# Partial Strassen products in the gate and feed-forward projections of a two-layer encoder trunk

## The chip, the cores and the metric

The kernel runs on one core of one Trainium2 chip. The metric is device time in microseconds. Engines are named as the profile does: PE is TensorE, PEld its weight loads, DVE VectorE, ACT ScalarE, POOL GpSimd, SP SyncE, whose queue issues most DMAs.

## The reference

Two layers (`DEPTH = 2`) work on a sequence of 256 rows of width 2048, all in float32. In each layer one input projection feeds three attention branches, the branches are merged by gates that are computed from the layer's input, and a feed-forward part follows:

```python
h = x @ w_in[l]                                   # 2048 -> 4608, split into the heads of A, B, C
ya, yb, yc = ...                                  # three attentions
ga, gb, gc = jnp.split(jax.nn.sigmoid(x @ w_gate[l] + b_gate[l]), 3, axis=-1)     # 2048 -> 6144
mix = ga * (ya @ w_br_a[l]) + gb * (yb @ w_br_b[l]) + gc * (yc @ w_br_c[l])
x = layer_norm(DEEPNORM_ALPHA * x + mix @ w_out[l], ln1_g[l], ln1_b[l])
f_gate, f_up = jnp.split(x @ w_ffn_in[l], 2, axis=-1)                             # 2048 -> 2 x 5632
x = layer_norm(DEEPNORM_ALPHA * x + (jax.nn.silu(f_gate) * f_up) @ w_ffn_out[l], ln2_g[l], ln2_b[l])
```

## The kernel before

The 256 rows are two row tiles of 128. Each matrix product is cut into blocks of 512 output columns (`CW`) and k-tiles of 128; two k-tiles by 512 columns of a weight are one *unit* (`UK = 2`), a DMA of 512 KB into one of five `raw` buffers. `split_unit` cuts a unit into a rounded part and a rest, both of the type that TensorE takes at its full rate: ScalarE casts `raw` to `wh`, VectorE subtracts to get `wl`, with six buffers each. The activations are split the same way (`xh`, `xl`; `rh`, `rl`). A product of a row tile, a k-tile and a block is then three matmuls of 128x128 by 128x512: high by high, high by low, low by high. `gemm` does that for 16 k-tiles and two row tiles, 96 matmuls, into two PSUM banks `acc`, of which there are four; four more banks (`aux`) take transposes and small products.

The program is written with tiles, and a planner orders the instructions of each engine when the program is built: from the order in the text, the dependencies and durations that it estimates. An engine then works through its own list in that order. The attention work is written as generators in the list `side`; `pump` runs one step of the first of them after each unit of a `gemm`, and `drain` runs all that are left.

In the feed-forward part the first hidden block uses two plain `gemm` calls; the other ten blocks use `pair_gemm`, which makes the two column blocks (gate and up) together. Seen as two rows of tiles times two columns of blocks, k-tiles are taken four at a time as a 2x2 by 2x2 product, which Strassen's scheme does in seven products in place of eight. Before the change the first four k-tiles are one such *seven* with two k-tiles to a quarter, k-tiles 4 and 5 are a *seven* with one k-tile to a quarter, and the other ten are plain, `four`. The sums of x that the scheme needs are made once for a layer by `x_sums`; the sums of weights are made for each pair by VectorE:

```python
hub = act.tile([P, UK, CW], F32, tag=("rh3", "rl3")[turn[0]], name="hub")
nc.sync.dma_start(hub, block(src, k1, n2))
...
nc.vector.tensor_add(u, hub, w22)
nc.vector.tensor_add(hub, hub, w11)
nc.vector.tensor_add(u, u, w11)
nc.vector.tensor_add(u, u, w21)
```

A pair has seven banks, four of `acc` (`p3`, `p7`, `q5`, `q4`) and three of `aux` (`p1`, `p6`, `p2`); `todo` counts the products of each, 3 for `p1`, `p6`, `p7` and 13 for the others. At its end VectorE combines the banks to the four results (lines 660 to 667), ScalarE and VectorE make silu and the product, and TensorE transposes the hidden block (`hidTp`, line 136) for the product with `w_ffn_out`, which follows after each group of two or three blocks.

The gates are plain: for each of three branches and four blocks a `gemm` with `w_gate`, bias and sigmoid, and a `gemm` with the branch's weight (8, 4 and 4 k-tiles). In the last branch the mixed block is transposed (`mixTp`) right behind it. At the very start x comes in four chunks of 512 columns; each is loaded, transposed, cast by ScalarE and subtracted by VectorE when the first `gemm` comes to it, so the first product meets all four chunks in turn.

Of the kernel before, what the change touches and what calls it, by code (L numbers as in the profile page):

```python
# [33 lines left out]
def trunk_kernel(ctx: ExitStack, tc: tile.TileContext, x, w_in, sinks, lq1, lk1, lq2, lk2, diff_g,  # L34
# [16 lines left out]
    def split(h, l, src, scale=None):  # L51

        if scale is None:
            nc.scalar.copy(h, src)  # L54
            nc.vector.tensor_sub(l, src, h.bitcast(F32))  # L55
# [12 lines left out]

    def split_unit(raw):
# [3 lines left out]
        nc.scalar.copy(h[:, 0:n], raw)  # L73
        nc.vector.tensor_sub(l[:, 0:n], raw, h[:, 0:n].bitcast(F32))  # L74
        return h, l
# [17 lines left out]

    def gemm(src, kw0, nk, c0, lhs, tail=0):
# [24 lines left out]

    def tmp(name):  # L120
# [4 lines left out]

    def bcast(vec, c0, name):
        t = scr.tile([P, CW], F32, tag="bc", name=name, bufs=4)
        nc.gpsimd.dma_start(t, vec[c0:c0 + CW].partition_broadcast(P))
        return t
# [16 lines left out]
    def set_x(c, t, src):  # L146
# [3 lines left out]
        split(xh[c][t], xl[c][t], pv)  # L150

    def x_lhs(kt, t):
        c = kt // 4
        if xh[c][t] is None:
            x0 = [tmp("x0") for _ in range(NT)]
            for u in range(NT):
                nc.sync.dma_start(x0[u], x[0, u * P:(u + 1) * P, c * CW:(c + 1) * CW])
            for u in range(NT):
                set_x(c, u, x0[u])
# [15 lines left out]
    for layer in range(DEPTH):  # L175
# [48 lines left out]
        def v_heads(acc, col0, slots):  # L224
            for i, s in enumerate(slots):
                for t in range(NT):
                    nc.scalar.copy(s[:, t * P:(t + 1) * P], acc[t][:, col0 + i * P:col0 + (i + 1) * P])

# [111 lines left out]
        acc = gemm(wi, 0, 16, 1024, x_lhs)  # L340
# [10 lines left out]
        sink = const.tile([P, AQ], F32, tag="sink", name="sink")  # L351
        nc.sync.dma_start(sink, sinks[layer].partition_broadcast(P))
        nsink = const.tile([P, AQ], F32, tag="nsink", name="nsink")
        nc.vector.tensor_scalar_mul(nsink, sink, -1.0)

        lv = const.tile([P, 4, 64], F32, tag="lv", name="lv")
        for i, v in enumerate((lq1, lk1, lq2, lk2)):
            nc.sync.dma_start(lv[:, i, :], v[layer].partition_broadcast(P))
        lp = const.tile([P, 2, 64], F32, tag="lp", name="lp")
        nc.vector.tensor_mul(lp, lv[:, 0::2, :], lv[:, 1::2, :])  # L360
        ls = const.tile([P, 2], F32, tag="ls", name="ls")
        nc.vector.tensor_reduce(ls, lp, AX.X, ALU.add)
        le = const.tile([P, 2], F32, tag="le", name="le")
        nc.scalar.activation(le, ls, AF.Exp)
        lam = const.tile([P, 1], F32, tag="lam", name="lam")
        nc.vector.tensor_sub(lam, le[:, 0:1], le[:, 1:2])
        nc.vector.tensor_scalar_add(lam, lam, lam_init)

        gcol = const.tile([P, 1], F32, tag="gcol", name="gcol")
        nc.sync.dma_start(gcol, diff_g[layer].rearrange("(p o) -> p o", o=1))  # L370
        nc.vector.tensor_scalar_mul(gcol, gcol, 1.0 - lam_init)
# [3 lines left out]
        relb = const.tile([P, NHC, 3 * P], F32, tag="relb", name="relb")  # L375
        for h in range(NHC):
            raw = tmp("hank")[:, :SEQ]
            row = rel_bias[layer, h]
            nc.sync.dma_start(raw, bass.AP(row.tensor, row.offset + 129, [[1, P], [1, SEQ]]))
            nc.vector.tensor_add(relb[:, h, 0:P], raw[:, 0:P][:, ::-1], mask_b[:, 0:P])  # L380
            nc.vector.tensor_add(relb[:, h, P:3 * P], raw[:, ::-1], mask_b[:, P:3 * P])
# [3 lines left out]
        acc = gemm(wi, 0, 16, 0, x_lhs)  # L385
# [31 lines left out]

        mix = [[None] * NT for _ in range(NCH)]
        mixT = [None] * NCH
        for b, (wbr, nk, y0i) in enumerate(((w_br_a, 8, 0), (w_br_b, 4, 2), (w_br_c, 4, 3))):  # L420
# [4 lines left out]
            for c in range(NCH):  # L425
                bg = bcast(b_gate[layer], b * D + c * CW, "bg")
                acc = gemm(w_gate[layer], 0, 16, b * D + c * CW, x_lhs)
                gs = []
                for t in range(NT):
                    g = tmp("gate")  # L430
                    nc.vector.tensor_add(g, acc[t], bg)
                    nc.scalar.activation(g, g, AF.Sigmoid)
                    gs.append(g)
                if b == 0 and c == 0:
                    drain()
                acc = gemm(wbr[layer], 0, nk, c * CW, y_lhs)
                for t in range(NT):
                    if b == 0:
                        mix[c][t] = act.tile([P, CW], F32, tag=f"fb{c * NT + t}", name=f"mix{c}{t}")
                        nc.vector.tensor_mul(mix[c][t], gs[t], acc[t])  # L440
                    else:
                        nc.vector.tensor_mul(gs[t], gs[t], acc[t])
                        nc.vector.tensor_add(mix[c][t], mix[c][t], gs[t])
                if b == 2:
                    mixT[c] = ychunk(c)
                    for t in range(NT):
                        pv = transpose4(mix[c][t], "mixTp")
                        s = slice(t * P, (t + 1) * P)
                        split(mixT[c][0][:, :, s], mixT[c][1][:, :, s], pv)
# [66 lines left out]


        sums = {}
        turn = [0]

        def sum_tiles():
            pair = const.tile([P, 2, 4, P], F32R, tag="relb", name="sums")
            for i in range(6):
                yield act.tile([P, 4, P], F32R, tag=f"fa{i}", name="sums")
            for i in range(2):
                yield pair[:, i]
            while True:
                yield scr.tile([P, 4, P], F32R, tag="bc", name="sums", bufs=4)

        def x_sums(delay):  # L530


            yield from wait(delay)
            tiles = sum_tiles()
            for c in range(NCH):
                z = []
                for t in range(NT):
                    v = tmp("z").rearrange("p (k q) -> p k q", k=4)
                    nc.vector.tensor_add(v, xh[c][t].bitcast(F32), xl[c][t].bitcast(F32))
                    z.append(v)  # L540
                yield
                n = (2, 1, 0, 0)[c]
                if n:
                    a11, a12, a21, a22 = (v[:, j:j + n, :] for v in z for j in (0, n))
                    p = tmp("zs").rearrange("p (k q) -> p k q", k=4)
                    q = tmp("zs").rearrange("p (k q) -> p k q", k=4) if n == 2 else p[:, 2:4]
                    s1, s2, s3, s4 = p[:, 0:n], p[:, n:2 * n], q[:, 0:n], q[:, n:2 * n]
                    nc.vector.tensor_sub(s1, a21, a22)
                    nc.vector.tensor_sub(s3, a11, a21)
                    nc.vector.tensor_sub(s2, a11, s1)  # L550
                    yield
                    nc.vector.tensor_sub(s4, a12, s2)
                    parts = [p, q] if n == 2 else [p]
                else:
                    nc.vector.tensor_sub(z[0], z[0], z[1])
                    parts = [z[0]]
                got = []
                for v in parts:
                    h, l = next(tiles), next(tiles)
                    split(h, l, v)  # L560
                    got.append((h, l))
                    yield
                if n == 1:
                    nc.vector.tensor_sub(z[0][:, 2:4], z[0][:, 2:4], z[1][:, 2:4])
                    hl = next(tiles)
                    split(hl[:, 0:2], hl[:, 2:4], z[0][:, 2:4])
                    got.append((hl[:, 0:2], hl[:, 2:4]))
                    yield
                sums[c] = got

        def pair_gemm(src, n1, n2):

            bank = {}  # L580
            for k in ("p3", "p7", "q5", "q4"):
# [172 lines left out]
```

## Time and profile before

| | |
|---|---|
| time before, median of 3 runs | 2830.11 us (2830.01 to 2830.28) |
| the profiled execution: its own time | 2827.89 us |
| its span, first to last instruction | 2826.0 us |
| PE busy | 2791.0 us, 99%, 12660 matmuls and transposes |
| PEld busy | 2296.8 us, 81% |
| DVE busy | 1966.3 us, 70%, 2282 instructions |
| ACT busy | 1349.6 us, 48% |
| POOL busy | 60.7 us, 2% |
| DMA | 549.20 MB, 194 GB/s on average |

Busy time is the time in which at least one instruction of the engine runs; matmuls overlap, so a busy PE may still be waiting in part, and the distance between the starts of two matmuls says more. The profiled execution is one of its own and has its own time; the median is of other executions.

### The profile page before, as it was taken

To read this page: it belongs to the slowest core of one execution; us is meant where nothing else is said; L and a number is where in the kernel's file an instruction comes from. 1 tells how busy PE (TensorE), PEld (TensorE's weight loads), DVE (VectorE), ACT (ScalarE), POOL (GpSimd) and SP (SyncE) were. 2 spreads that over 40 slices of the span, in tenths; PEclk is the share of its full clock that TensorE was granted. 3 is DMA by queue.
4 is the path that set the end of the run, shared out by engine and by line. 5 is a ranking of instruction groups with operands and counts; after the bars stand their busy time and mean duration, and the time that the engine had idled before them with its cause. 6 is when DMAs were issued, how large, how long until landed. Compare 5 with 4: busy or idle time off the path is not lost. (4 is left out here: it accounts for less than half of the span.)

```text
span 2826.0 us, 33866 instructions
## 1 busy us (share of the span) xinstructions
PE 2791.0 (99%) x12660; PEld 2296.8 (81%) x12660; DVE 1966.3 (70%) x2282; ACT 1349.6 (48%) x1722; POOL 60.7 (2%) x110
## 2 busy tenths in 40 slices
PE   8999999999999999999999999999999999999998
PEld 6887888887888888888878888888878888888886
DVE  5656555566986877868776565555579779688686
ACT  4455444443554544545445454444435545455452
POOL 0000000000000000000000000000000000000000
PEclk9999999999999999999999999999999999999999
DMA  7555666665665666665764556666656656656564
GB/s 255 171 164 175 202 200 205 203 209 177 198 204 190 194 202 193 194 201 177 229 216 153 179 177 202 201 204 202 209 162 214 200 190 196 203 186 208 186 198 141
DMA packets 282660, 549.20 MB, mean 194 GB/s; under 512 B 19840, under 2 KB 21376, under 8 KB 282496
## 3 DMA queue, kind: packets, MB, share of 16 engines
q1 hardware_dynamic: 276096, 526.07, 58.1%
q0 software_dynamic: 6400, 20.98, 2.6%
q8 instruction: 99, 1.62, 0.2%
q14 instruction: 65, 0.53, 0.1%
HBM read 542.78 MB, written 4.19 MB: 194 GB/s over the span
## 5 line engine op out<-in xcount | busy, mean ns | idle before, releaser
L74 DVE TENSOR_TENSOR wl<-raw,wh 128x1024 fp32r<-128x1024 f32 x972 | 1182.6, 1223 | 718.0 <-ACT wh L73 713.6
L73 ACT CAST wh<-raw 128x1024 fp32r<-128x1024 f32 x972 | 1019.2, 1054 | 1239.1 <-PE acc L104 809.4
L102 PE MATMUL acc<-wh,xh 128*128 128x512 f32 x1472 | 582.2, 396 | 6.9 <-ACT xh L54 6.9
L103 PE MATMUL acc<-wl,xh 128*128 128x512 f32 x1472 | 575.8, 391 | 3.6 <-DVE wl L74 2.0
L104 PE MATMUL acc<-wh,xl 128*128 128x512 f32 x1472 | 576.2, 392 | 0.2 <-DVE xl L55 0.2
L103 PE MATMUL acc<-wl,rh 128*128 128x512 f32 x1216 | 474.3, 390 | 0.0
L102 PE MATMUL acc<-wh,rh 128*128 128x512 f32 x1216 | 473.8, 390 | 0.0
L104 PE MATMUL acc<-wh,rl 128*128 128x512 f32 x1216 | 473.7, 390 | 0.0
L102 PEld LDWEIGHTS acc<-wh,xh 128*128 128x128 f32 x1472 | 277.1, 188 | 66.2 <-ACT xh L54 9.1
L103 PEld LDWEIGHTS acc<-wl,xh 128*128 128x128 f32 x1472 | 277.3, 188 | 61.9 <-DVE wl L74 4.1
L104 PEld LDWEIGHTS acc<-wh,xl 128*128 128x128 f32 x1472 | 277.0, 188 | 59.6 <-DVE xl L55 2.2
L102 PEld LDWEIGHTS acc<-wh,rh 128*128 128x128 f32 x1216 | 228.3, 188 | 47.3
L103 PEld LDWEIGHTS acc<-wl,rh 128*128 128x128 f32 x1216 | 228.3, 188 | 47.2
L104 PEld LDWEIGHTS acc<-wh,rl 128*128 128x128 f32 x1216 | 228.3, 188 | 46.9
L595 PE MATMUL q<-wh,xl 128*128 128x512 f32 x460 | 179.2, 390 | 0.0
L591 PE MATMUL q<-wh,xh 128*128 128x512 f32 x460 | 179.1, 389 | 0.0
L593 PE MATMUL q<-wl,xh 128*128 128x512 f32 x460 | 179.0, 389 | 0.0
L595 PE MATMUL p<-wh,sums 128*128 128x512 f32 x380 | 149.0, 392 | 0.0
L591 PE MATMUL p<-wh,sums 128*128 128x512 f32 x380 | 148.9, 392 | 0.0
L593 PE MATMUL p<-wl,sums 128*128 128x512 f32 x380 | 147.8, 389 | 0.0
L74 DVE TENSOR_TENSOR wl<-u,wh 128x1024 fp32r<-128x1024 f32 (+1 forms) x100 | 111.4, 1114 | 37.2 <-ACT wh L73 37.2
L73 ACT CAST wh<-u 128x1024 fp32r<-128x1024 f32 (+1 forms) x100 | 96.7, 967 | 78.6 <-PE p L595 39.8
(184 smaller groups left out, 2509.1 us busy)
## 6 DMA issues: line engine op xcount, KB each, us to landing
raw<-in_w_ffn_in_dram SPq DMA_DIRECT2D x332, 512.0 KB, 3.6
raw<-in_w_gate_dram SPq DMA_DIRECT2D x192, 512.0 KB, 4.2
raw<-in_w_ffn_out_dram SPq DMA_DIRECT2D x176, 512.0 KB, 3.7
raw<-in_w_in_dram SPq DMA_DIRECT2D x144, 512.0 KB, 3.6
raw<-in_w_out_dram SPq DMA_DIRECT2D x64, 512.0 KB, 4.0
raw<-in_w_br_a_dram SPq DMA_DIRECT2D x32, 512.0 KB, 4.1
hub<-in_w_ffn_in_dram SPq DMA_DIRECT2D x20, 512.0 KB, 3.4
raw<-in_w_br_b_dram SPq DMA_DIRECT2D x16, 512.0 KB, 4.6
```

The source lines that it names most:

```text
L73: nc.scalar.copy(h[:, 0:n], raw)
L74: nc.vector.tensor_sub(l[:, 0:n], raw, h[:, 0:n].bitcast(F32))
L102: nc.tensor.matmul(acc[t], ah, wh[:, j, :], start=kt == 0, stop=False)
L103: nc.tensor.matmul(acc[t], ah, wl[:, j, :], start=False, stop=False)
L104: nc.tensor.matmul(acc[t], al, wh[:, j, :], start=False, stop=kt == nk - 1)
L591: nc.tensor.matmul(bank[k], ah, wh[:, j, :], start=k not in begun, stop=False)
L593: nc.tensor.matmul(bank[k], ah, wl[:, j, :], start=False, stop=False)
L595: nc.tensor.matmul(bank[k], al, wh[:, j, :], start=False, stop=todo[k] == 0)
```

## The change

Five things change; the result is the same but for rounding.

- `w_ffn_in`: k-tiles 0 to 3 and 8 to 11 are sevens (`FF`), the rest plain. In each seven two of the four weight sums (`hub` + `w11` and `u` + `w21`) are no longer made by VectorE: a DMA on GpSimd's queue loads the weight again and adds it to what is there (`accum_op`). The half seven is no longer used.
- `w_gate`: five of the six pairs of gate blocks in a layer use `pair_gemm` with one seven (`GATE`) and all four weight sums on VectorE. The bias, loaded into a `raw` buffer, is added while the banks are combined. The first pair stays plain, and `x_sums` runs beside it.
- The transposes of the hidden blocks and of the mixed blocks are put into the list `later` and issued in the next product, after its second unit.
- At the start the first two column blocks of `w_in` are made together (`first_gemms`): each chunk of x feeds 48 matmuls in place of 24. The first chunk is cast by VectorE in place of ScalarE, and `issue_after` puts the first weight casts or subtractions behind the casts of x, and the setup of constants behind the last split, on the engine's list.
- The banks and the plain units of a pair are used in another order.

```diff
+    def run_later():
+        while later:
+            later.pop(0)()
...
     def gemm(src, kw0, nk, c0, lhs, tail=0):
...
+            if k == 2:
+                run_later()
             pump()
...
+    def first_gemms(src, c0, c1):
+        accs = [[psA.tile([P, CW], F32, tag="acc", name="acc") for _ in range(NT)] for _ in range(2)]
+        loaded = load_x(0)
+        for c in range(NCH):
+            behind[:] = loaded
+            for acc, col in zip(accs, (c0, c1)):
+                for k in (4 * c, 4 * c + 2):
+                    wh, wl = load_unit(src, k, col)
...
+                if col == c0 and c + 1 < NCH:
+                    loaded = load_x(c + 1, mm.ins)
+        return accs
...
-    def set_x(c, t, src):
+    def set_x(c, t, src, first=False):
...
-        split(xh[c][t], xl[c][t], pv)
+        if not first:
+            return split(xh[c][t], xl[c][t], pv)
+        h = nc.vector.tensor_copy(xh[c][t], pv)
+        return h.ins, nc.vector.tensor_sub(xl[c][t], pv, xh[c][t].bitcast(F32)).ins
...
+            def seven(c, fill):
...
+                if hubs:
+                    hub = act.tile([P, UK, CW], F32, tag=hubs[c // 2], name="hub")
+                    nc.sync.dma_start(hub, block(src, k1, n2))
+                else:
+                    hub = load_raw(src, k1, n2)
+                w22 = load_raw(src, k2, n2)
+                u = scr.tile([P, UK, CW], F32, tag="att", name="u", bufs=2)
+                nc.vector.tensor_add(u, hub, w22)
+                fours(0)
+                prod("p7", s3, split_unit(u))
+                prod("p3", s4, split_unit(w22))
+                w11 = load_raw(src, k1, n1)
+                if hubs:
+                    nc.gpsimd.dma_start(hub, block(src, k1, n1), accum_op=ALU.add)
+                else:
+                    nc.vector.tensor_add(hub, hub, w11)
+                nc.vector.tensor_add(u, u, w11)
+                fours(1)
+                prod("p1", a11, split_unit(w11))
+                fours(2)
+                if not hubs:
+                    prod("q5", s1, split_unit(hub))
+                    fours(3)
+                prod("p6", s2, split_unit(u))
+                w21 = load_raw(src, k2, n1)
+                if hubs:
+                    nc.gpsimd.dma_start(u, block(src, k2, n1), accum_op=ALU.add)
+                    fours(3)
+                else:
+                    nc.vector.tensor_add(u, u, w21)
+                fours(4)
+                prod("p2", a12, split_unit(w21))
+                if hubs:
+                    prod("q5", s1, split_unit(hub))
+                fours(5)
+                prod("q4", a22, split_unit(u))
+                fours(6)
...
+            elif kinds[2] == "7":
+                seven(0, [N2[0:1], N2[1:2], [], [], N2[4:5], N1[0:1], []])
+                seven(2, [N2[5:6], N1[1:2], [], [], [], N1[4:], []])
+            else:
+                seven(0, [N2[0:1], N2[1:2], N2[2:3], N2[3:4], N2[4:], N1[0:1], N1[1:2]])
+                if load_bias:
+                    bias = load_bias()
+                for f in N1[2:]:
+                    four(*f)
...
+            if not load_bias:
+                nc.scalar.copy(p1, bank["p1"])
+            else:
+                nc.vector.tensor_add(p1, bank["p1"], bias[0])
+                nc.vector.tensor_add(bias[1], bias[0], bias[1])
...
-        acc = gemm(wi, 0, 16, 1024, x_lhs)
+        if layer == 0:
+            acc, acc_q = first_gemms(wi, 1024, 0)
+        else:
+            acc = gemm(wi, 0, 16, 1024, x_lhs)
...
+        GATE = ("7", "4", "4", "4")
+        FF = ("7", "4", "7", "4")
...
+                if b == 0 and c0 == 0:
+                    bgs = load_bias()
+                    side.append(x_sums(sums, GATE, 0))
...
+                    drain()
+                else:
+                    gates = pair_gemm(w_gate[layer], *cols, sums, GATE, load_bias)
...
-                    accg, accu = pair_gemm(w_ffn_in[layer], f * CW, FFN + f * CW)
+                    accg, accu = pair_gemm(w_ffn_in[layer], f * CW, FFN + f * CW, sums, FF, hubs=("rh3", "rl3"))
...
+                later.append(transposed_hid)
```

`four` is as before, but counts the pair's plain units and issues what is in `later` at the second; `N2` and `N1` are the plain units of k-tiles 4 to 15 in the second and the first column block.

## Rows read from the trace of the kernel before

**Rows 1.** The page: busy time by engine; granted clock, in tenths, in 40 slices.
```profile
PE 2791.0 (99%) x12660; PEld 2296.8 (81%) x12660; DVE 1966.3 (70%) x2282; ACT 1349.6 (48%) x1722; POOL 60.7 (2%) x110
...
PEclk9999999999999999999999999999999999999999
```

**Rows 2.** Timeline of TensorE: start us, duration us, line, operation.
```profile
27.17 0.39 PE L103 MATMUL acc<-wl,xh 128*128 128x512 f32 x1
...
34.88 0.39 PE L104 MATMUL acc<-wh,xl 128*128 128x512 f32 x1
```

**Rows 3.** Groups by shape: count, then busy us, mean ns, idle before.
```profile
L74 DVE TENSOR_TENSOR wl<-raw,wh 128x1024 fp32r<-128x1024 f32 x972 | 1182.6, 1223 | 718.0 <-ACT wh L73 713.6
...
L626 DVE TENSOR_TENSOR u<-u,raw 128x1024 f32<-128x1024 f32 x20 | 24.4, 1221 | 0.2
...
L661 DVE TENSOR_TENSOR v<-p,p 128x512 f32<-128x512 f32 x20 | 13.7, 684 | 0.0
...
L74 DVE TENSOR_TENSOR wl<-u,wh 128x512 fp32r<-128x512 f32 x20 | 13.7, 687 | 0.0
```

**Rows 4.** Stretches, as the second line names the columns.
```profile
core 0: us, PE busy (x) PEld busy (x) DVE busy (x) ACT busy (x) POOL busy (x), PEclk, DMA share, GB/s
544.00:632.00 88.00, 88.00 (x400) 72.44 (x399) 53.43 (x58) 39.84 (x44) 4.93 (x9) 1.00 0.65 211
466.00:493.00 27.00, 27.00 (x121) 22.35 (x120) 15.56 (x17) 11.59 (x12) 0.55 (x1) 1.00 0.67 208
520.00:549.00 29.00, 29.00 (x133) 23.88 (x132) 17.71 (x20) 12.85 (x15) 0.55 (x1) 1.00 0.64 203
700.00:744.60 44.60, 43.28 (x194) 34.52 (x193) 42.99 (x61) 21.68 (x27) 1.58 (x2) 1.00 0.57 183
897.50:1091.00 193.50, 192.96 (x862) 159.18 (x861) 150.56 (x159) 97.46 (x102) 0.00 (x0) 1.00 0.60 196
1091.20:1217.60 126.40, 126.40 (x566) 104.35 (x565) 109.19 (x118) 69.92 (x74) 0.00 (x0) 1.00 0.63 203
10.00:20.00 10.00, 6.68 (x14) 4.38 (x15) 5.47 (x6) 4.53 (x7) 0.00 (x0) 1.00 1.04 390
```

**Rows 5.** Waits of TensorE: us in total, times, longest.
```profile
PE acc L102 <- ACT xh L54: 6.9, 2, 4.3
...
PE hidTp L136 <- DVE sig L691: 3.2, 5, 1.1
```

**Rows 6.** Line 494, the residual loads on GpSimd's queue, 256 KB each.
```profile
L494 POOL DMA_DIRECT2D xres<-in_x_dram x8: 548/548/548, 550.8 to 629.3; - x8
...
DMA to landing us min/median/max: 3.4/4.2/5.5
```

**Rows 7.** Line 66, the weight loads on SyncE's queue, 512 KB each.
```profile
L66 SPq DMA_DIRECT2D raw<-in_w_ffn_in_dram x332: 367/368/596, 668.6 to 2744.9; - x166
...
DMA to landing us min/median/max: 3.3/3.9/11.9
```

**Rows 8.** Timeline of the start.
```profile
3.34 1.60 POOL L128 DMA_DIRECT2D bg<-in_b_gate_dram  x3
...
4.36 1.94 PE L136 MATMUL xTp<-ident,x 128*128 128x128 f32 x8 [4.36 <-DMA x<-in_x_dram]
...
6.32 1.04 ACT L73 CAST wh<-raw 128x1024 fp32r<-128x1024 f32 x1 [4.30 <-DMA raw<-in_w_in_dram]
...
10.65 0.80 PE L102 MATMUL acc<-wh,xh 128*128 128x512 f32 x1 [4.35 <-ACT xh L54]
...
14.18 1.04 ACT L73 CAST wh<-raw 128x1024 fp32r<-128x1024 f32 x1 [3.58 <-DMA raw<-in_w_in_dram]
...
17.21 0.63 PE L104 MATMUL acc<-wh,xl 128*128 128x512 f32 x1
...
18.06 0.63 PE L103 MATMUL acc<-wl,xh 128*128 128x512 f32 x1
...
20.14 0.39 PE L104 MATMUL acc<-wh,xl 128*128 128x512 f32 x1
```

More of the change, by code (lines that the diff above doesn't have):

```diff
@@ L1 @@
 import math
[L2 removed]
+from contextlib import ExitStack, nullcontext
 import concourse.bass as bass
@@ L67, in load_raw @@
         return raw
+    split_ins = []
+    behind = []
     def split_unit(raw):
@@ L72, in split_unit @@
         n = raw.shape[1]
-        nc.scalar.copy(h[:, 0:n], raw)
-        nc.vector.tensor_sub(l[:, 0:n], raw, h[:, 0:n].bitcast(F32))
+        a, v = behind.pop(0) if behind else (None, None)
+        with tc.issue_after(a) if a else nullcontext():
+            nc.scalar.copy(h[:, 0:n], raw)
+        with tc.issue_after(v) if v else nullcontext():
+            split_ins.append(nc.vector.tensor_sub(l[:, 0:n], raw, h[:, 0:n].bitcast(F32)).ins)
         return h, l
@@ L227, in v_heads, with sum_tiles, x_sums @@
                     nc.scalar.copy(s[:, t * P:(t + 1) * P], acc[t][:, col0 + i * P:col0 + (i + 1) * P])
+        def sum_tiles():
+            pair = const.tile([P, 2, 4, P], F32R, tag="relb", name="sums")
+            for i in range(6):
+                yield act.tile([P, 4, P], F32R, tag=f"fa{i}", name="sums")
+            for i in range(2):
+                yield pair[:, i]
+            for i in range(4):
+                yield scr.tile([P, 4, P], F32R, tag="bc", name="sums", bufs=4)
+        def x_sums(sums, kinds, delay):
+            yield from wait(delay)
+            tiles = sum_tiles()
+            for c, kind in enumerate(kinds):
+                z = []
+                for t in range(NT):
+                    v = tmp("z").rearrange("p (k q) -> p k q", k=4)
+                    nc.vector.tensor_add(v, xh[c][t].bitcast(F32), xl[c][t].bitcast(F32))
+                    z.append(v)
+                yield
+                n = {"7": 2, "74": 1, "4": 0}[kind]
+                if n:
+                    a11, a12, a21, a22 = (v[:, j:j + n, :] for v in z for j in (0, n))
+                    p = tmp("zs").rearrange("p (k q) -> p k q", k=4)
+                    q = tmp("zs").rearrange("p (k q) -> p k q", k=4) if n == 2 else p[:, 2:4]
+                    s1, s2, s3, s4 = p[:, 0:n], p[:, n:2 * n], q[:, 0:n], q[:, n:2 * n]
+                    nc.vector.tensor_sub(s1, a21, a22)
+                    nc.vector.tensor_sub(s3, a11, a21)
+                    nc.vector.tensor_sub(s2, a11, s1)
+                    yield
+                    nc.vector.tensor_sub(s4, a12, s2)
+                    parts = [p, q] if n == 2 else [p]
+                else:
+                    nc.vector.tensor_sub(z[0], z[0], z[1])
+                    parts = [z[0]]
+                got = []
+                for v in parts:
+                    h, l = next(tiles), next(tiles)
+                    split(h, l, v)
+                    got.append((h, l))
+                    yield
+                if n == 1:
+                    nc.vector.tensor_sub(z[0][:, 2:4], z[0][:, 2:4], z[1][:, 2:4])
+                    hl = next(tiles)
+                    split(hl[:, 0:2], hl[:, 2:4], z[0][:, 2:4])
+                    got.append((hl[:, 0:2], hl[:, 2:4]))
+                    yield
+                sums[c] = got
@@ L383, in trunk_kernel @@
         qk_heads(acc, 256, ak, "a")
         v_heads(acc, 256, av)
-        acc = gemm(wi, 0, 16, 0, x_lhs)
+        acc = acc_q if layer == 0 else gemm(wi, 0, 16, 0, x_lhs)
         qk_heads(acc, 512, aq[0:4], "a")
@@ new lines, in trunk_kernel, with load_bias, transposed_mix @@
+            for c0 in range(0, NCH, 2):
+                cols = [b * D + c * CW for c in (c0, c0 + 1)]
+                def load_bias(cols=cols):
+                    t = wpool.tile([P, 2, CW], F32, tag="raw", name="bg", bufs=5)
+                    for i, c in enumerate(cols):
+                        nc.gpsimd.dma_start(t[:, i], b_gate[layer][c:c + CW].partition_broadcast(P))
+                    return t[:, 0], t[:, 1]
+                if b == 0 and c0 == 0:
+                    bgs = load_bias()
+                    side.append(x_sums(sums, GATE, 0))
+                    gates = []
+                    for c, bg in zip(cols, bgs):
+                        acc = gemm(w_gate[layer], 0, 16, c, x_lhs)
+                        gates.append([tmp("gate") for _ in range(NT)])
+                        for t in range(NT):
+                            nc.vector.tensor_add(gates[-1][t], acc[t], bg)
+                    drain()
+                else:
+                    gates = pair_gemm(w_gate[layer], *cols, sums, GATE, load_bias)
+                for gs in gates:
+                    for g in gs:
+                        nc.scalar.activation(g, g, AF.Sigmoid)
+                for c, gs in zip((c0, c0 + 1), gates):
+                    acc = gemm(wbr[layer], 0, nk, c * CW, y_lhs)
+                    for t in range(NT):
+                        if b == 0:
+                            mix[c][t] = act.tile([P, CW], F32, tag=f"fb{c * NT + t}", name=f"mix{c}{t}")
+                            nc.vector.tensor_mul(mix[c][t], gs[t], acc[t])
+                        else:
+                            nc.vector.tensor_mul(gs[t], gs[t], acc[t])
+                            nc.vector.tensor_add(mix[c][t], mix[c][t], gs[t])
+                    if b == 2:
+                        def transposed_mix(c=c):
+                            for t in range(NT):
+                                pv = transpose4(mix[c][t], "mixTp")
+                                s = slice(t * P, (t + 1) * P)
+                                split(mixT[c][0][:, :, s], mixT[c][1][:, :, s], pv)
+                        mixT[c] = ychunk(c)
+                        later.append(transposed_mix)
@@ L530, in x_sums @@
[L530 to L569, printed above, removed]
```

290 lines of the change are left out of this document (130 added, 160 removed).

## The prediction

> **What bounds the kernel now.** I read the page first. TensorE is busy for 2791.0 of 2826.0 us, 99%, and its clock is granted in full throughout [rows 1]. A busy matmul row can hide a slow one, since matmuls overlap, so the second view was the timeline: two 512-column matmuls 34 steps apart start 34.88 - 27.17 = 7.71 us apart, 0.2268 us each, while one lasts 0.39 us [rows 2]. The same step comes out of the windows: three pair steps of 183 matmuls each fill 126.4 us [rows 4], 549 x 0.2268 = 124.5 us plus the transposes between. So TensorE issues back to back, and an instruction less on it is 0.2268 us less of the end, if nothing else becomes late. The third view, the waits of TensorE, says how little is lost now: 6.9 us at the start for the first x tiles, 3.2 us for the transposes of the hidden state [rows 5]. VectorE is what could become late: 70% on average [rows 1], but 86% in the pair steps (109.19 of 126.4) and 96% in the first part of the feed-forward (42.99 of 44.6), where TensorE yet works 43.28 us [rows 4].
>
> The profiled execution took 2827.9 us, 1.9 us outside the span; the median is 2830.1 and the runs differ by 0.3. I work out savings in the profiled execution and take them off the median. Under 0.2%, 5.7 us, I call no change.
>
> **Matmuls removed.** Before, a pair of feed-forward column blocks takes 61 products of three matmuls (3 + 13 + 13 + 3 + 3 + 13 + 13, the `todo` of its banks), 183. After it, two full sevens of two k-tiles each give 4 + 4 + 4 + 4 x 12 = 60, 180. There are 10 pairs in each of two layers: 3 x 20 = 60 matmuls. Two gate columns took 2 x 96 = 192; a gate pair takes 3 x 2 + 4 x 14 = 62 products, 186; with five pairs in a layer 6 x 10 = 60 more. 120 x 0.2268 = **27.2 us**. This term I trust to a microsecond: the matmuls that stay have the same shape and step.
>
> **VectorE and ScalarE in the feed-forward.** A pair goes from 20 and a half splits to 22, and loses four 512-column sums: 2 x 1.22 for two more whole splits, less 0.69 for the half one and 4 x 0.68 for the sums, -1.0 us [rows 3]. VectorE worked 150.56 us in a group of three pairs and its four output products; the products alone are 24 splits and 8 adds, 34.7 us, so a pair costs 38.6 now and 37.6 then. TensorE has 42.1 - 0.7 = 41.4 us for it. The slack is 3.8 us a pair. Two of the four weight sums of each seven move to DMAs that add; without that VectorE would have 42.5 us and be the bound, so the cover is needed.
>
> **The adding DMAs** are what the trace does not show. Their issue is on GpSimd, idle 98% of the time [rows 1]. The first sum (`hub`) has some nine VectorE instructions between its release and its split, 11 us. The second (`u`) has four splits, 4 x 1.22 = 4.9 us if VectorE is in full run, more when TensorE paces it. Behind a late `u`, ScalarE and VectorE stand in order, so the splits of the next pair's weights are late next, then TensorE, after the six weight buffers (6 x 42.1/22 = 11.5 us) are used up. Bounds for issue to landing: below, the shortest 512 KB load from SP's queue, 3.3 us; above, the longest, 11.9 us [rows 7]. My value: a 256 KB load from GpSimd's queue takes 4.2 us at the median [rows 6]; the other 256 KB at the 390 GB/s that the start reached [rows 4] add 0.7, and a second pass to read what is added to 1.3: **6.2 us**. It is nearest to the GpSimd row because queue and neighbours are the same. Then 1.3 us of each seven is exposed, 2.6 us a pair, inside the slack of 3.8: **0 us**. The extra bytes: 20 instead of 16 blocks of 0.524 MB in 41.4 us, 253 GB/s, 304 if the adding ones count twice; 390 was reached. The Trainium skill, page "DMA: Bandwidth & Descriptors", section "Anatomy of one DMA", gives for a DMA from this queue about 2.0 us plus its bytes over 436 GB/s; by it, as an estimate, the add would land in 3.2 us, nothing would be exposed, and the sum would be the same with more room. For the 256 KB load it gives 2.6 us where the row has 4.2, so here it is too short, and the sum goes by the row.
>
> **Gate pairs.** Two gate-and-branch columns cost VectorE 2 x 15.56 us in 54 [rows 4]. A pair adds three splits (3.7), four sums (4.9) and six ops of the epilogue (4.1): 43.8 in 52.6 us, 83%; in the last branch, where the mix is transposed, 2 x 17.71 + 12.7 = 48.1 in about 56.6, 85%. The feed-forward pairs run at 86% with TensorE never waiting, so I put 0; the epilogue's last two adds stand behind the pair's last matmul, but the banks that the next product needs (`q5`, `p3`, `p7`) are done 48 matmuls, 10.9 us, before. Lower bound 0, upper 1.4 us a pair (both adds), 14 us in all. The sums of x for the gates, four sets of about 3 us, lie in 43 us of plain gate products in which VectorE is 58% busy: 0. The bias takes one of five `raw` buffers: SP waits on buffers anyway, 0.
>
> **Start.** In the first 20 us TensorE does 14 big matmuls between 10.65 and 20.14 us; it waits for ScalarE, whose casts of weights stand ahead of the casts of x, and for weights, while the DMA engines are full (1.04 of their time, 390 GB/s) [rows 4, 8]. Each x chunk feeds 24 matmuls, 5.4 us. After the change it feeds 48, 10.9 us, for five blocks of 0.5 MB: 240 GB/s, below the 390, and the four early bias loads are gone. The x cast moves to VectorE: the transposes end at 6.3, four ops of 0.69 us to 9.1, the first `wl` at 10.3, and from there TensorE has work without a break. The step there is 0.43 us (17.21 to 18.06 is two of them) and turns to 0.23 just before 20.14, though the row of the stretch gives a granted clock of 1.00, 2.4 GHz; I keep 4 us of slow steps, and then 9 + 25 = 34 matmuls are done by 20.14, 20 more than now, **4.5 us**. Bounds: 0 (third weight block as late as now, 14.2 us) and 9 (start at 7.0 and full step).
>
> **Transposes later.** They are issued behind the second unit of the next product, so the inputs have 5 us more. That saves the 3.2 us of [rows 5]; bounds 0, where the planner had moved them already, and 5. **3.2 us**.
>
> **First two products at once** use all four banks of `acc`, so the third product needs the rope of the first to be done; it has 24 matmuls, 5.4 us, for about 3.5 us of VectorE. I put 2 us of loss, 0 to 4. The drain before the branch products comes one column later; nothing waits there longer than now.
>
> Sum: 27.2 + 4.5 + 3.2 - 2 = 32.9; 2830.1 - 32.9 = **2797 us**, a ratio of 0.988.
>
> **Rivals.** (1) *The add lands late*: slower. With y the exposed time of a seven, a group loses 2y - 3.8 for each pair, less 11.5 of lead: 6y - 22.9 for three pairs, 4y - 19.1 for two, and with two groups of each in each of two layers 40y - 168. It eats 32.9 us at y = 5.0, a landing of 9.9 us; at 11 us, y = 6.1, it costs 76: 2873. For it: 11.9 us was seen; VectorE has little slack. Against: that was with the DMA engines full, and here they are busy 0.6 of their time now [rows 4] and about 0.8 with the bytes added. GpSimd's issues take 548 ns, shortest and longest alike [rows 6], with VectorE 61% busy beside them (53.43 of 88) [rows 4]; an issue that had to wait out one VectorE instruction would add 1.22 us, a landing of 7.4, still under 9.9. The Trainium skill, page "SBUF — State Buffer", section "Who interferes with whom", tells of such a wait, on the ports that the two engines share, and speaks against issuing DMAs from GpSimd beside VectorE work in its two-port modes; the two-input ops of this kernel it leaves out of that. The even 548 ns agree. (2) *The gate pairs give nothing back*: 1.4 us lost at each of ten pairs cancels their 13.6: 2811. For: VectorE from 58% to 85%. Against: the feed-forward's 86%. (3) *The DMA engines fill*: only if an adding DMA costs four plain ones, 32 blocks in 41.4 us, 405 GB/s against 390; then a pair takes 43.0, 1.6 us more, 32 in all: no change, 2829. (4) *The removal doesn't show*, since the planner reorders and TensorE waits elsewhere: the same 2829.
>
> **How the numbers follow.** Forecast with its bounds (2786 to 2808): 0.63. Rival 2 or a partial late add, 2808 to 2824: 0.19. Rivals 3 and 4, 2825 to 2835: 0.06. Rival 1: 0.12. The best of all bounds, 27.2 + 9 + 5 with no loss, gives 2789, so the range begins at 2787 and ends at 2824; it leaves out 0.18 above, the last two cases, and about 0.02 below. Faster 0.82, no change 0.06, slower 0.12.
>
> **What would show it.** TensorE's instructions 12660 - 120 = 12540, its busy time 27 us less. The adding DMAs land in 5 to 8 us, and no wait of a split for them lasts over 2 us; waits of TensorE in the pair steps stay under 1 us. By 20 us over 30 big matmuls are done. Waits for the hidden state's transposes vanish. The prediction is wrong if splits of `u` wait 5 us or more, VectorE comes to 95% in the pair steps, or TensorE shows gaps behind `wl`.

## The result, and the profile after

The changed kernel takes 2856.98 us (2856.15 to 2860.99) against 2830.2 of the kernel before on the same chip: a ratio of 1.0097, interval 1.008 to 1.0115. It is slower by 1%, where 2797 and faster was forecast, and it lies above the range. The profiled execution took 2860.99 us. Its page, first the busy time, then the granted clock in 40 slices, then the software queue, which is GpSimd's:

```profile
PE 2786.9 (97%) x12540; PEld 2283.2 (80%) x12540; DVE 2076.0 (73%) x2392; ACT 1394.5 (49%) x1780; POOL 157.7 (6%) x190
...
PEclk9999999999999999999999999999999999999998
...
q0 software_dynamic: 28160, 62.92, 11.6%
```

TensorE has the 120 instructions less that were counted (12660 in [rows 1]), but its busy time fell by 4.1 us where 27 was expected, and its share fell from 99% to 97%: it now waits, and some steps are slow. The waits (us in total, times, longest):

```profile
ACT wh L78 <- DMA u<-in_w_ffn_in_dram: 170.1, 33, 9.4
...
ACT wh L78 <- DMA hub<-in_w_ffn_in_dram: 26.1, 12, 3.0
...
PE acc L115 <- DVE v L460: 16.5, 8, 2.7
...
PE q L342 <- DVE wl L80: 13.3, 23, 1.3
```

The first line is the one that the prediction named as its refutation: splits of `u` wait for the adding DMA, 33 times of 40, 5.2 us each on average and up to 9.4. The third says what follows on TensorE: at 8 places, the ends of the 8 groups of pairs, it waits for `v`, a sum of the epilogue. Line 400, the adding DMA of `u`, by itself:

```profile
L400 POOL DMA_DIRECT2D u<-in_w_ffn_in_dram x40: 1194/1203/1575, 739.0 to 2781.6; - x40
...
who waited for it (us, times):
  ACT wh L78: 170.1, 33
...
DMA to landing us min/median/max: 5.9/8.5/11.0
```

It lands after 8.5 us at the median where 6.2 was taken; the issue holds GpSimd for 1.2 us where the 256 KB load of [rows 6] took 0.55. The end of one group of pairs shows how that reaches TensorE (timeline: start us, duration us, engine, line, operation; in brackets how long the engine had been idle, and what ended it):

```profile
1206.28 1.20 POOL L400 DMA_DIRECT2D u<-in_w_ffn_in_dram  x1 [7.02 <-DVE wl L80]
...
1208.17 2.35 DVE L80 TENSOR_TENSOR wl<-raw,wh 128x1024 fp32r<-128x1024 f32 x2
...
1214.55 1.05 ACT L78 CAST wh<-u 128x1024 fp32r<-128x1024 f32 x1 [6.02 <-DMA u<-in_w_ffn_in_dram]
...
1215.63 1.23 DVE L80 TENSOR_TENSOR wl<-u,wh 128x1024 fp32r<-128x1024 f32 x1 [5.10 <-ACT wh L78]
...
1216.77 0.68 DVE L458 TENSOR_TENSOR v<-p,p 128x512 f32<-128x512 f32 x1
...
1219.03 0.39 PE L344 MATMUL q<-wh,xl 128*128 128x512 f32 x1
...
1220.24 0.68 DVE L460 TENSOR_TENSOR v<-q,v 128x512 f32<-128x512 f32 x1
...
1221.07 0.47 PE L115 MATMUL acc<-wh,rh 128*128 128x512 f32 x1 [1.65 <-DVE v L460]
...
1222.70 0.80 PE L115 MATMUL acc<-wh,rh 128*128 128x512 f32 x1 [0.70 <-DVE c L463]
...
1224.15 0.63 PE L115 MATMUL acc<-wh,rh 128*128 128x512 f32 x1
1224.58 0.63 PE L116 MATMUL acc<-wl,rh 128*128 128x512 f32 x1
```

After the issue VectorE has 4.2 us of splits left (to 1210.52), the window that the prediction read; then it stands 5.10 us. Behind `u`, in order, stand the sums of the epilogue that free the banks. TensorE finishes the pair at 1219.03 and can't begin `w_ffn_out` until line 460 has read its bank. Inside a group of pairs TensorE waits for the late split itself, here for the rest `wl` of `u`:

```profile
995.08 1.23 DVE L80 TENSOR_TENSOR wl<-u,wh 128x1024 fp32r<-128x1024 f32 x1 [5.25 <-ACT wh L78]
...
996.36 0.50 PE L342 MATMUL q<-wl,xh 128*128 128x512 f32 x1 [0.76 <-DVE wl L80]
```

The stretches of the same kernel show the rest (the first line names the columns):

```profile
core 0: us, PE busy (x) PEld busy (x) DVE busy (x) ACT busy (x) POOL busy (x), PEclk, DMA share, GB/s
686.26:1426.75 740.49, 718.06 (x3159) 585.19 (x3157) 557.24 (x590) 363.53 (x390) 55.47 (x52) 0.99 0.74 219
2102.37:2846.88 744.51, 721.04 (x3158) 586.52 (x3157) 555.62 (x588) 358.67 (x385) 54.91 (x50) 0.99 0.71 213
1091.64:1221.07 129.43, 125.89 (x558) 102.47 (x556) 102.82 (x105) 70.26 (x76) 13.20 (x11) 1.00 0.81 230
1222.70:1225.40 2.70, 2.70 (x6) 2.16 (x7) 2.70 (x4) 2.12 (x3) 0.00 (x0) 0.50 0.75 276
1226.00:1229.00 3.00, 3.00 (x15) 2.40 (x14) 3.00 (x5) 1.57 (x2) 0.00 (x0) 1.00 0.60 191
```

The first two rows are the two feed-forwards, from the first large matmul to the last. In the kernel before they were:

```profile
695.13:1412.83 717.70, 714.16 (x3188) 587.38 (x3187) 569.75 (x629) 357.55 (x380) 8.13 (x14) 1.00 0.61 198
2095.59:2813.30 717.71, 714.15 (x3189) 587.38 (x3187) 565.52 (x619) 352.34 (x375) 6.19 (x10) 1.00 0.59 191
```

So they lost 49.6 us together. The third row after answers to the pair step of [rows 4]: 129.4 us, with VectorE at 79% where it was at 86%; it has less to do and still stops TensorE. The fourth is what follows the two waits of the timeline: the granted clock is 0.50, 1.2 GHz, and a step takes 0.43 us (1224.15 to 1224.58); 0.6 us later it is 1.00 again, 2.4 GHz. Elsewhere the change gave what it should: the rest of layer 1, from its first large matmul to the first of its feed-forward, takes 673.6 us (1428.80 to 2102.37) where it took 680.7 (1414.89 to 2095.59), 7.1 less, for 6.8 of gate matmuls; the start gained 3.2 us (the 192nd large matmul begins at 60.40, before at 63.58).

### The profile page after: what moved, and what is told of

Same layout as the page of the kernel before. It is cut to its first block, busy times and chain, and to the rows that moved or that the text cites. A ratio compares the mean times of both kernels' runs of the same rounds, so it can differ in the third digit from the quotient of the medians.

```text
span 2859.1 us, 34118 instructions
## 1 busy us (share of the span) xinstructions
PE 2786.9 (97%) x12540; PEld 2283.2 (80%) x12540; DVE 2076.0 (73%) x2392; ACT 1394.5 (49%) x1780; POOL 157.7 (6%) x190
## 5 line engine op out<-in xcount | busy, mean ns | idle before, releaser
L115 PE MATMUL acc<-wh,rh 128*128 128x512 f32 x1216 | 483.2, 398 | 21.0 <-DVE v L460 16.5
L115 PE MATMUL acc<-wh,xh 128*128 128x512 f32 x768 | 307.2, 401 | 0.0
L116 PE MATMUL acc<-wl,xh 128*128 128x512 f32 x768 | 300.7, 392 | 3.5 <-DVE wl L80 1.9
L117 PE MATMUL acc<-wh,xl 128*128 128x512 f32 x768 | 301.0, 392 | 0.0
L80 DVE TENSOR_TENSOR wl<-u,wh 128x1024 fp32r<-128x1024 f32 x150 | 183.0, 1220 | 144.9 <-ACT wh L78 143.5
L78 ACT CAST wh<-u 128x1024 fp32r<-128x1024 f32 x150 | 157.6, 1051 | 256.8 <-DMA u<-in_w_ffn_in_dram 170.1
L342 PE MATMUL q<-wl,xh 128*128 128x512 f32 x660 | 259.6, 393 | 13.5 <-DVE wl L80 13.3
L340 PE MATMUL p<-wh,sums 128*128 128x512 f32 x580 | 225.8, 389 | 0.2 <-DVE sig L802 0.2
L344 PE MATMUL p<-wh,sums 128*128 128x512 f32 x580 | 225.8, 389 | 0.0
L342 PE MATMUL p<-wl,xh 128*128 128x512 f32 x480 | 187.3, 390 | 2.9 <-DVE wl L80 2.9
L340 PE MATMUL p<-wh,xh 128*128 128x512 f32 x480 | 188.2, 392 | 0.0
L344 PE MATMUL p<-wh,xl 128*128 128x512 f32 x480 | 187.0, 389 | 0.0
```

The costliest lines, as they stand in the source:

```text
L80: split_ins.append(nc.vector.tensor_sub(l[:, 0:n], raw, h[:, 0:n].bitcast(F32)).ins)
L115: nc.tensor.matmul(acc[t], ah, wh[:, j, :], start=kt == 0, stop=False)
L116: nc.tensor.matmul(acc[t], ah, wl[:, j, :], start=False, stop=False)
L117: nc.tensor.matmul(acc[t], al, wh[:, j, :], start=False, stop=kt == nk - 1)
L340: nc.tensor.matmul(bank[k], ah, wh[:, j, :], start=k not in begun, stop=False)
L342: nc.tensor.matmul(bank[k], ah, wl[:, j, :], start=False, stop=False)
```

## The experiments

My theory after this, A: the add of `u` lands later than the splits between its issue and its own, and ScalarE and VectorE, which go in order, hold the epilogue and the next splits behind it. Rivals: B, the second full seven gives VectorE too much; C, the added bytes make all loads late; D, an adding DMA disturbs the engines wherever it stands. Diffs are against the changed kernel. The kernel before took 2833.4 to 2834.1 us at the median on the chips of the experiments, so differences to the changed kernel are taken between ratios, times 2833; each interval is some 4 us either way.

**Both sums on VectorE.**

```diff
-                    nc.gpsimd.dma_start(hub, block(src, k1, n1), accum_op=ALU.add)
-                    nc.gpsimd.dma_start(u, block(src, k2, n1), accum_op=ALU.add)
+                nc.vector.tensor_add(hub, hub, w11)
+                nc.vector.tensor_add(u, u, w21)
```

> All four weight sums of a feed-forward seven on VectorE, no adding DMA; the rest is the changed kernel. Theory A (the add into u lands after 8.5 us against a window of 4.9 us, ScalarE and VectorE stand behind it in order, and the pair's last banks come free late): the 170 us of waits of casts for u are gone, and so are the waits of TensorE at the pair ends; VectorE has 42.5 us a pair against 41.4 of TensorE, which the lead over three pairs covers: 2800 us, 2795 to 2812. Theory B (two whole sevens in a pair are too much for VectorE and the order of banks, whoever makes the sums): as slow as the changed kernel or slower, 2850 to 2880. Theory C (the extra 42 MB slow the weight loads of SP): loads land as before in 3.6 us, 2800.

Measured 2790.68 us, ratio 0.9847 [0.983, 0.9863]: (1.0097 - 0.9847) x 2833 = 71 us below the changed kernel, and the two feed-forwards, 707.1 and 707.2 us, make all of it (740.5 and 744.5 above, 70.7 us more). It is 4 us below the range that A gave. Page and stretches (both feed-forwards, then the pair step as above):

```profile
PE 2759.1 (99%) x12540; PEld 2276.7 (82%) x12540; DVE 2164.8 (78%) x2472; ACT 1410.5 (51%) x1780; POOL 60.3 (2%) x110
```

```profile
688.29:1395.43 707.14, 705.05 (x3158) 582.52 (x3157) 601.82 (x630) 371.54 (x390) 7.07 (x12) 1.00 0.63 200
2071.50:2778.68 707.18, 705.13 (x3158) 582.56 (x3157) 599.34 (x628) 366.50 (x385) 6.18 (x10) 1.00 0.61 194
1077.83:1201.91 124.08, 124.08 (x556) 102.74 (x555) 118.78 (x120) 74.54 (x78) 0.00 (x0) 1.00 0.64 201
```

VectorE is at 96% of the pair step (118.78 of 124.08), 39.6 us a pair, and TensorE shows no wait in this step. B falls: the adds needed no cover.

**One of the two by DMA.** The same replacement for `u` alone, then for `hub` alone.

> The sum of hub by the adding DMA, the sum of u by VectorE. Theory A: the hub add has some 11 us, ScalarE waited only 26 us for it in all; VectorE has 40.0 us a pair, under 41.4: 2797 us, 2793 to 2810. Theory B: over 2840. Theory C: half of the extra traffic stays, half of the 60 us lost stays: about 2827.

> The sum of u by the adding DMA, the sum of hub by VectorE. Theory A: the late add stays and VectorE has one more instruction in its window, so the window is 6.1 us in place of 4.9, but VectorE has 1.2 us more work a seven: 2840 to 2865. Theory C: half of the traffic, about 2827. Theory B: 2850 to 2880.

With only `hub` added by DMA 2790.78 us, 0.9848 [0.9833, 0.9862]; with only `u` 2908.2 us, 1.0263 [1.0248, 1.0279]. In the first the `hub` add lands late too, but one split alone waits for it:

```profile
ACT wh L78 <- DMA hub<-in_w_ffn_in_dram: 1.3, 1, 1.3
```

```profile
hub<-in_w_ffn_in_dram POOLq DMA_DIRECT2D x40, 512.0 KB, 7.9
```

In the second:

```profile
raw<-in_w_ffn_in_dram SPq DMA_DIRECT2D x312, 512.0 KB, 3.9
...
u<-in_w_ffn_in_dram POOLq DMA_DIRECT2D x40, 512.0 KB, 8.2
```

```profile
PE q L342 <- DVE wl L80: 24.3, 35, 1.3
PE acc L115 <- DVE v L457: 21.5, 8, 2.7
```

The plain loads land after 3.9 us, as before [rows 7], and the kernel is yet the slowest of all: C falls as the cause. The same kind of DMA, landing equally late, costs nothing where eight VectorE instructions or more lie between its issue and its use (the timeline of the first), and everything where mostly four to six do (that of the second). That this kernel is slower than the one with both adds fits A (VectorE, with the `hub` sums back, has less room to make up a stall; 42 of the 47 us between the two lie inside the pairs), but it stands 43 us above the top of A's range, and that size is not explained.

**Plain loads in place of the adding ones**, at the same places; `hub` and `u` are overwritten, so their two sums are left out.

```diff
-                    nc.gpsimd.dma_start(u, block(src, k2, n1), accum_op=ALU.add)
+                    nc.gpsimd.dma_start(u, block(src, k2, n1))
```

> The two adding DMAs of a seven become plain loads into the same place from the same queue, so the sums are left out and the same bytes are read; every instruction list keeps its order. If the adding itself makes the landing long (8.5 us at the median for u, 7.5 for hub), it falls to about 5 us, the waits for u to under 40 us and the time to about 2805 to 2825. If the queue of GpSimd or the traffic makes it long, landing and time stay: 8 us, 2850 to 2860.

2814.98 us, 0.9934 [0.9919, 0.9948]. Line 400 there:

```profile
L400 POOL DMA_DIRECT2D u<-in_w_ffn_in_dram x40: 714/724/729, 739.8 to 2734.9; - x40
...
  ACT wh L78: 69.9, 19
...
DMA to landing us min/median/max: 4.2/5.8/10.2
```

So adding makes this DMA 2.7 us longer to land and its issue 0.48 us longer, and that is worth 46 us of the 71. The other 25 come with a landing of 5.8 us, below the 6.2 that I had taken for harmless; the waits for `u`, 69.9 us, are above the 40 that I had put. Of its profiled execution, 18.5 us above that of the kernel with both sums on VectorE, 11 lie in the products behind the groups of pairs and 2 in the pairs, and TensorE waits for the hidden state's transposes:

```profile
PE hidTp L166 <- DVE sig L802: 11.4, 7, 2.1
```

**A longer window, with both adding DMAs.** Plain units move between the add of `u` and its split: six and five splits in place of four.

```diff
-                seven(0, [N2[0:1], N2[1:2], [], [], N2[4:5], N1[0:1], []])
-                seven(2, [N2[5:6], N1[1:2], [], [], [], N1[4:], []])
+                seven(0, [N2[0:1], [], [], [], N2[1:2] + N2[4:5], N1[0:2], []])
+                seven(2, [[], [], [], [], N2[5:6], N1[4:], []])
```

> Both adding DMAs stay; only the order of the plain units changes: between the issue of the add into u and its split lie six splits in the first seven and five in the second, where there were four. At TensorE's pace (1.88 us a split) the window grows from 7.5 us to 11.3 and 9.4, against a landing of 8.5 at the median. Theory A (the late add stalls the queues): ScalarE's waits for u fall from 170 us to under 60, no longest over 6, the waits of the output products' banks for the epilogue vanish, and the time is 2790 to 2806, ratio 0.985 to 0.990. Rival D (adding DMAs disturb TensorE or VectorE by themselves, wherever they stand): the time stays over 2830.

2800.3 us, 0.9881 [0.9865, 0.9898]. The waits of ScalarE, line 400, and one full pair step (three pairs):

```profile
ACT wh L78 <- DMA u<-in_w_ffn_in_dram: 5.4, 5, 2.0
```

```profile
DMA to landing us min/median/max: 5.6/5.9/8.9
```

```profile
891.95:1015.92 123.97, 123.97 (x556) 102.85 (x555) 108.10 (x109) 74.56 (x77) 13.17 (x11) 1.00 0.88 251
```

170.1 us of waiting became 5.4, and the step takes the 124.0 us of the kernel without adding DMAs, with both in it and 251 GB/s moved. The order gives back 61 of the 71 us: A holds, and D doesn't in these steps. The landing fell too, to 5.9, so the order helped twice; but the plain load landed after 5.8 in the short window and cost 25 us, so the window has its own share. What is left lies at the first pair of each layer, where TensorE waited once for 2.4 and 2.9 us, by the profile for an `rl` of line 55. I took this for a sum of x. Two kernels asked for it: one begins the sums of x two steps earlier (`x_sums(sums, FF, 0)`), one has the new order with both sums on VectorE.

> The kernel with the longer window, but the sums of x for the feed-forward begin two steps earlier. There TensorE waited once in each layer 2.4 to 2.9 us for the split of such a sum, with a stretch of slow steps behind it; these two stretches took 9 us over those of the kernel with both sums on VectorE. If that is all that the longer window left, the wait goes and the time is 2791, ratio 0.985. If the adding DMAs still cost something, it stays at 2797 or above.

> The order of the longer window, but both sums on VectorE: no adding DMA at all. The kernel with the longer window (adding DMAs kept) stood 9.6 us above the one with both sums on VectorE in the old order, lost at the first pairs of each layer's feed-forward, and beginning the sums of x earlier did not bring it back (2800.4 where 2791 was expected). If those 9.6 us belong to the order, this kernel takes 2798 to 2803 (ratio about 0.988); if they belong to the adding DMAs, it takes 2790 to 2793 (0.985).

The first took 2800.42 us (0.9882 [0.9867, 0.9897]), where 2791 was expected: a miss. Its waits for `rl` fell from 5.7 to 3.5 us in all, but those for splits in the plain blocks ahead of the pairs rose from 1.9 to 5.3, so it doesn't tell what the wait for `rl` costs. The second took 2792.29 (0.9851 [0.9835, 0.9868]), so some 8 us do belong to the adding DMAs. The timeline of the kernel with the longer window, in its first pair, shows what I had misread:

```profile
748.67 1.22 DVE L381 TENSOR_TENSOR u<-hub,raw 128x1024 f32<-128x1024 f32 x1 [3.02 <-DMA raw<-in_w_ffn_in_dram]
...
754.36 1.28 DVE L55 TENSOR_TENSOR rl<-hidTp,rh 128x512 fp32r<-128x512 f32 x2
```

The `rl` is the split of the hidden state's transposes, and VectorE is late for it after 3.0 us of waiting for a plain weight load. With adding DMAs in this order these loads land after 5.3 us at the median, without them after 4.2: a small part of C, then, where the pairs begin. That this load alone makes the 8 us was not tried.

**The other parts**, each undone on the kernel with both sums on VectorE: one half seven in place of the second seven (`FF = ("7", "74", "4", "4")`, 183 matmuls, `hub` in a `raw` buffer as in the other kinds); plain gates, without `x_sums` for them; the transposes at once (`transposed_hid()` in place of `later.append(transposed_hid)`, the same for the mix); the first two products one after the other.

> A feed-forward pair goes back to one full seven and one half seven (183 matmuls, all weight sums by VectorE); the rest is the changed kernel. The adding DMAs are gone. If a matmul less is worth its 0.2268 us and nothing else, the second full seven is worth 13.6 us, so this kernel stands 13 to 14 us above the one with both sums on VectorE: ratio to before about 0.9895, 2803 to 2806 of 2833. If the second full seven costs VectorE or the DMA engines something that hides part of it, the two are nearer than 8 us: below 2799.

> The kernel with both sums on VectorE, but all gates go back to plain products (192 matmuls for two columns instead of 186, no sums of x for the gates). By the prediction's step the five pairs of each layer are worth 60 x 0.2268 = 13.6 us and cost nothing: 2804, ratio 0.9895. By its rival 2 they give nothing: 2791, ratio 0.985.

> The kernel with both sums on VectorE, but the transposes of the hidden state and of the mix are issued at once again. By the prediction's step, worth 3.2 us (bounds 0 and 5): ratio about 0.986, and the waits of TensorE for hidTp come back. By the stage times (the feed-forward gains 21 us against before where its matmuls give 13.6) the later transposes are worth up to 7 us: ratio 0.987.

> The kernel with both sums on VectorE, but the first two products run one after the other as before (weights' casts ahead of x's), the biases still late. If the start is worth what the traces of before and after show at the 192nd large matmul, 3.2 us, this one stands 3 us above the kernel with both sums on VectorE (ratio about 0.986) and its 192nd large matmul begins at 63 to 64 us; if the start's gain is given back behind it, by the four banks that it holds, the two are the same within 1 us.

The half seven took 2804.3 us (0.9895 [0.988, 0.991]): by the medians the second seven is worth 13.6 us, the price of its 60 matmuls. Plain gates took 2807.17 (0.9904 [0.9888, 0.9921]): the gate pairs are worth 16.5, their 13.6 within the interval, and rival 2 falls. Transposes at once took 2803.95 (0.9897 [0.9882, 0.9911]): 13.3 us for moving them, more than either expectation. Of its profiled execution, 16.7 us above that of the kernel with both sums on VectorE, 9.3 lie in the two feed-forwards (713.4 and 710.3 us). The waits for transposes:

```profile
PE hidTp L166 <- DVE sig L797: 5.9, 9, 2.0
PE mixTp L166 <- DVE mix L699: 5.5, 2, 3.9
```

The two products one after the other took 2791.66 us (0.985 [0.9835, 0.9865]), and the 192nd large matmul began at 60.65 (61.66 with them together): the pairing of the first products is worth nothing that can be seen. Then what gained the 3.2 us at the start? That kernel also lacks the four early bias loads of [rows 8], so I put four such loads back, unread:

```diff
+    for i in range(4):
+        early = scr.tile([P, CW], F32, tag="bc", name="early", bufs=4)
+        nc.gpsimd.dma_start(early, b_gate[0][i * CW:(i + 1) * CW].partition_broadcast(P))
```

> The kernel with the first two products one after the other (and both sums on VectorE), to which four loads of the bias from GpSimd's queue at the very start are added, unread, as the kernel before had them in its first microseconds. If their absence is what brought the third weight cast from 14.2 to 12.1 us and the 192nd large matmul from 63.6 to 60.7, both go back to within 0.7 us of the former and the time rises by about 3 us, ratio 0.986. If the gain comes from elsewhere, the cast stays at 12 to 12.8.

2794.35 us (0.9861 [0.9846, 0.9876]). The third weight cast, without the early loads, then with them:

```profile
12.14 1.04 ACT L78 CAST wh<-raw 128x1024 fp32r<-128x1024 f32 x1 [1.36 <-DMA raw<-in_w_in_dram]
```

```profile
15.13 1.04 ACT L78 CAST wh<-raw 128x1024 fp32r<-128x1024 f32 x1 [2.33 <-DMA raw<-in_w_in_dram]
```

The 192nd large matmul went from 60.65 to 64.67, 0.4 us further than the expectation's bound, and the time rose by 2.7, which alone would be inside the interval: 1 MB in a stretch where the DMA engines are full [rows 4] costs 4.0 us at that matmul. So leaving out these loads accounts for the 3.2 us of the start.

## Why the prediction was wrong

The step that failed is **the adding DMAs, 0 us**. They cost 71 us, and all of it goes with the second sum: alone the first costs nothing, the second 118. The window of the second sum was read rightly, 4.9 us against 4.2 in the timeline. Two things in the step were not.

The landing was mis-sized: 6.2 us taken, 8.5 measured. The plain 512 KB load from the same queue takes 5.8, and the adding itself 2.7, not the 1.3 of a second pass. The Trainium skill, page "DMA: Bandwidth & Descriptors", section "Anatomy of one DMA", by which I estimated 3.2 us, is further off than the row was: neither the plain load nor the adding one agrees here.

Worse, the break-even was wrong. Rival 1 had the right mechanism, yet its formula, 40y - 168, gives no loss at all for y = 8.5 - 4.9 = 3.6 us, and 33 us only at a landing of 9.9. It credited each group with 11.5 us of lead from the six weight buffers. At a group's end that lead does not protect: TensorE needs banks there, and the sums that free them stand on VectorE behind the late split. Inside a group there was none either: TensorE began on `u` as soon as its late split was done (996.36 above). And it counted no price for the clock behind a wait. Added up from the starts of matmuls in the two feed-forwards after, without the first 50 of each: 47.1 us over the usual step in 53 steps of 0.45 us or more (0.5 us in the kernel with both sums on VectorE), and 17.4 us in 120 slow steps of 0.30 to 0.45 (2.4); most of the rest lies at steps with transposes between. By place, the feed-forwards' 70.7 us over that kernel are 18 at the eight changes from pair to product, 29 in the products behind, where slow steps and late splits follow the wait, and 24 inside pairs. Even with 6.2 us the step would hardly have come to 0: the plain loads lose 25 us at 5.8. The chance of 0.12 for rival 1 was too small for a step on which everything stood.

The claim that **VectorE would be the bound without the cover**, 42.5 us a pair, was wrong too: 39.6 measured, under TensorE's 41.4. I had spread a whole group's VectorE work less the products' over the pairs, 38.6 each; the pair step of [rows 4] alone says 109.19 / 3 = 36.4. So the kernel ran adding DMAs where none were needed.

The terms around it held, were small or were put too low. **Matmuls removed**: 13.6 for the feed-forward as put, 16.5 for the gates where 13.6 was put, 12540 instructions as counted. **Gate pairs** cost nothing that can be seen, as said. **Start**: 3.2 us against 4.5, but for another reason; 26 large matmuls had begun by 20.14, not 34, since the third weight cast came at 11.33 and TensorE waited 3.2 us for it. The upper bound of 9 is nearer 10 by its own working, which changes nothing. The granted clock reads 1.00 there too, with steps of 0.43 us (13.45 to 13.88); behind the waits in the feed-forward the same step stood at 0.50, so for the first 20 us that row can't be taken for the clock. **Transposes later**: 13.3 us against 3.2 and a bound of 5. The waits of [rows 5], 3.2 us in the kernel before, were taken for the price; in the kernel with the other changes and the transposes at once they are 11.4 (5.9 and 5.5). Which of the changes lengthens them was not told apart. In the changed kernel the waits for `hidTp` stayed (6.1 us, by the profile for line 802 of VectorE, whose list stood behind `u`); with both sums on VectorE they are gone. **First two products**, a loss of 2 us: none seen. Without the adding DMA of `u` the sum of 32.9 us would have been 10 too small: the kernel with both sums on VectorE gains 42.7 (2833.43 to 2790.68), so rival 4 falls too. The parts one by one, 13.6 + 16.5 + 13.3 + 3.2, come to 46.6, the same within the intervals.

Rival 3 falls with the longer window, which moves 251 GB/s in the step shown, and that takes no longer than without the adding DMAs. The port of rival 1 doesn't show: the shortest issue of the `u` add takes 1194 ns, the median one 1203, the longest 1575, so none waited out a VectorE instruction of 1.22 us. The Trainium skill, page "SBUF — State Buffer", section "Who interferes with whom", leaves two-input ops out of its warning about DMA issues, and the trace agrees.

The kernel with both sums on VectorE, 2790.68 us, and the one with only the `hub` add on a DMA, 2790.78, beat both kernels; 0.1 us doesn't tell them apart.

## What to carry to other kernels

A transfer in the middle of an in-order list is priced by its landing against the work that truly lies between issue and use, and by what stands behind it on the same list: here not the next splits, but the sums that free PSUM banks. Buffers gave no lead here at a point where TensorE needed something else from the stalled engine. Before moving work off an engine that looks full, measure whether it stops the one that sets the end; here it ran at 96% and did not.

## What the runs showed of the hardware

- A 512 KB DMA from GpSimd's queue that adds to its destination landed after 8.5 us at the median in one place and 5.9 in another (the longer window), the plain one after 5.8 in the first; its issue took 1.20 us of GpSimd against 0.72.
- After waits of 1.65 and 0.70 us with three matmuls between them, TensorE's granted clock was 0.50 for 2.7 us, 1.2 GHz, and then 1.00 again. In the two feed-forwards 47.1 us in long steps came with 17.4 us in slow ones.
- VectorE at 96% of a 124 us step did not make TensorE wait once.
